# c in eight rows, turned and spread on chip, and 480 of 1920 low columns on GpSimd, in the first pass of a two-layer decoder

## Chip, core and metric

One core of a Trainium2 chip. The metric is the device time of one execution in microseconds; the kernel before takes 760.21 us (median of 3 runs, 759.72 to 760.39). The engines of the core run side by side and wait for each other through semaphores: TensorE (PE in the profile; PEld are its weight loads), VectorE (DVE), ScalarE (ACT), GpSimd (POOL) and SyncE (SP), which here issues most DMAs.

## What is computed

A decoder of two layers on one sequence of 256 tokens and width 1024, in float32. Each layer has a token mixer (layer 0: a mixture of three dilated attentions with 16 heads; layer 1: gated linear attention) and a gated convolutional FFN. Before each of them the input is normalised and modulated by shift and scale worked out from a conditioning vector `c`:

```python
mod = jax.nn.silu(c) @ w_ada[i] + b_ada[i]
sh1, sc1, g1, sh2, sc2, g2 = [m[:, None, :] for m in jnp.split(mod, 6, axis=-1)]
h = rmsnorm(x, norm_mix[i]) * (1.0 + sc1) + sh1
...
qkv = (h @ w_in).reshape(B, S, A_GROUPS, 3, A_HEADS, A_HEAD_DIM)
```

The change touches only the beginning: `silu(c)`, the norm of `x`, the first shift and scale, and the first part of `h @ w_in`.

## The kernel before

Everything is kept turned: channels on the 128 partitions, the 256 tokens along the free dimension, so `x` is eight tiles of 128 x 256 (`x_all`, `KT` = 8). A product of two float32 matrices is made from split operands: `hi` is the value rounded to a shorter format (`fp32r`), `lo` = value - `hi`, and three products hi·hi, lo·hi, hi·lo are summed (`mm3`, L200). For each weight tile ScalarE writes `hi` (a cast, `split`, L176) and VectorE writes `lo` (a subtraction of two SBUF operands, L182, or `low_part`, L188).

*Start (L85-126, L386-412).* `c` arrives as one row of 1024 numbers on one partition; two products with a row of ones (L125) spread it over all partitions, and ScalarE applies Silu from PSUM into `c_bc`, 128 x 1024, with the same numbers on every partition. Meanwhile `x` arrives in two halves, VectorE and ScalarE square it, VectorE adds the eight squares to two, TensorE sums over the channels, and ScalarE makes `rstd` from it through Ln and Exp (`rstd_of`, L212). Between these TensorE runs products that nobody reads (`keep_warm`, L297) and the six small products of the position bias (`rows`, L409).

*First pass (L415-440 and L673-685).* For each of the eight channel tiles `kt`:
- `ada_load` loads 128 x 2048 of `w_ada`, and two `ada_dot` (L138) on VectorE multiply one half each by `c_bc` and sum along the row; ScalarE turns each result into a shift or scale (`mod`, L150 or L152).
- `normed` (L282): VectorE writes `xr` = x · scale · rstd (L287), ScalarE `hhi` = round(xr + shift) (L289), VectorE `hlo` (L291).
- `split(..., lows=False)` (L165) loads 128 x 1920 of `w0`, and ScalarE casts two halves of 960; `low_part` (L185) is called once for each half on VectorE, the first behind `xr`, the second behind `hlo`.
- TensorE multiplies: 12 blocks of 128 columns for queries and keys (three products each, 256 columns) and a block of 384 for the values, for two halves of the tokens.

So VectorE's queue for one tile is: dot, dot, `xr`, low half, `hlo`, low half. Tiles 0 to 7 follow each other in it; `last` carries the order from tile to tile. The copies of `rows` from PSUM to SBUF (L437) stand on ScalarE behind the last cast of tile 0 (`copied[0]`).

*Order.* A scheduler places the instructions of each engine; `behind(i)` (L275) makes an instruction stand behind `i` in the queue of the same engine, and nothing between engines: real waits come from data and from buffers. A buffer of a pool is given out again once everything that uses it is done. PSUM has eight banks under three tags: 2 of `p`, 3 of `s`, 3 of `t`. `bank` (L74) takes the tag it is told, or the next from the cycle `p s t p s t s t`. Weight tiles have four raw buffers and three each for `hi` and `lo`.

Of the kernel before, what the change touches and what calls it, by code (L numbers as in the profile page):

```python
# [59 lines left out]
def trunk(ctx: ExitStack, tc: tile.TileContext, I, out):  # L60
# [16 lines left out]

    mm = nc.tensor.matmul

    def exp_ln_after(last):  # L80
        with tc.issue_after(last.ins):
            nc.scalar.preload_act_table_set(EXP_LN)


    c_row = wspl.tile([P, 2048], F32, tag="whi", name="c_row")  # L85
    nc.scalar.dma_start(c_row[:1, :D], I["c"])

    x_all = state.tile([P, KT, T], F32, name="x_all")
    x = [x_all[:, kt, :] for kt in range(KT)]

# [10 lines left out]
    def col(at):  # L101
        return small[:, at : at + 1]

    ones_d = const.tile([P, P], F32, name="ones_d")
    nc.vector.memset(ones_d, 1.0 / D)
    eps = const.tile([P, 1], F32, name="eps")
    nc.vector.memset(eps, EPS)
    ident = const.tile([P, P], F32, name="ident")
# [10 lines left out]
                                              op0=ALU.add, op1=ALU.mult)  # L119


    c_bc = const.tile([P, D], F32, name="c_bc")
    for n in range(2):
        ps = bank("cb", "t")
        last_c = mm(ps, ones_d[:1, :], c_row[:1, 512 * n : 512 * n + 512], start=True, stop=True)  # L125
        silu = nc.scalar.activation(c_bc[:, 512 * n : 512 * n + 512], ps, AF.Silu, scale=float(D))


    mod = {}
# [5 lines left out]
            nc.sync.dma_start(raw[:, c], I["w_ada"][l, n][:, c])  # L135
        return raw

    def ada_dot(l, n, s, raw):  # L138
# [3 lines left out]
        i = nc.vector.tensor_tensor_reduce(  # L142
            w, w, c_bc, op0=ALU.mult, op1=ALU.add, scale=1.0, scalar=0.0, accum_out=dot,
        )
        m = state.tile([P, 1], F32, tag=f"mod{l}{piece}{kt}", name="mod")
        b = col(C_BADA + 48 * l + 8 * piece + kt)
        if piece in (1, 4):
            g = col((C_NMIX if piece == 1 else C_NFFN) + 8 * l + kt)
            b1 = (16 if piece == 4 else 0) + 8 * l + kt
            j = nc.scalar.activation(m, dot, AF.Identity, scale=g, bias=one_b[:, b1 : b1 + 1])  # L150
# [120 lines left out]
    chain = {}  # L271
    squared = [None, None]

    @contextmanager
    def behind(*those):  # L275

        with ExitStack() as st:
            for i in those:
                st.enter_context(tc.issue_after(i.ins))
            yield  # L280

    def normed(l, sub, r, kt, first=(), between=None):  # L282

        xr = tmp.tile([P, T], F32, tag="xr", name="xr")
# [8 lines left out]
            )  # L293
        chain[kt] = chain[7] = i, j
        return h_hi[kt], h_lo[kt]

    def keep_warm(n):  # L297

        ps = bank("warm")
        for i in range(n):  # L300
            mm(ps[:, :P], ones_d, ones_d, start=True, stop=True)
# [82 lines left out]


    sq = wspl.tile([P, 2048], F32, tag="wlo", name="sq").rearrange("p (k t) -> p k t", k=KT)  # L386
    with behind(last_c):
        keep_warm(4)
    nc.vector.tensor_tensor(sq[:, 0:4, :], x_all[:, 0:4, :], x_all[:, 0:4, :], op=ALU.mult)
    with behind(silu):  # L390
        for i in (4, 6):
            last_sq = nc.scalar.activation(sq[:, i : i + 2, :], x_all[:, i : i + 2, :], AF.Square)
    for n in (0, 4):
        for m in (2, 1):
            last_add = nc.vector.tensor_tensor(sq[:, n : n + m, :], sq[:, n : n + m, :], sq[:, n + m : n + 2 * m, :], op=ALU.add)
        if n == 0:
            with behind(last_add):
                last_add = scale_terms(0)
    exp_ln_after(last_sq)
    r = rstd_of([sq[:, 0, :], sq[:, 4, :]])  # L400

    rows_ps, at = [], 0
    with behind(norm_ops[0]):
        keep_warm(3)
        for i, (g, n) in enumerate(ROWS):
            c = slice(at, at + n)
            ps = bank("rows", "t")[:16, 0:n]
            rows_ps.append((ps, c))
            last_row = mm(ps, tab[:, 16 * g : 16 * g + 16], oh[:33, c], start=True, stop=True)  # L409
            at += n  # L410
    with behind(last_row):
        keep_warm(6)


    w0, h = [], []  # L415
    last = last_add
    for kt in range(KT):
        ada = ada_load(0, kt, 1 if kt else 2)
        with behind(*((last,) if kt else (norm_ops[1], last))):
            dots = [ada_dot(0, kt, 0, ada)]  # L420
        with behind(dots[0][0]):
            dots.append(ada_dot(0, kt, 1, ada))

        def between(scaled, high):

            ahead, term = (dots[1][1], dots[1][1]) if kt == 0 else (dots[0][1], dots[1][1])
            w0.append(split(I["w0"][kt], 15 * P, 1 if kt else 2, after=((ahead,), (high,)), lows=False))
# [4 lines left out]
        with behind(chain[kt][1]):  # L432
            last = low_part(w0[kt], 1)
        if kt == 0:
            with behind(copied[0]):
                for ps, c in rows_ps:
                    nc.scalar.copy(rows[:, c], ps)  # L437
        if kt == 1:
            with behind(last):
                last = scale_terms(1)  # L440
# [35 lines left out]


    last_t, last_po, evacuated = [None], [None], []
    exps, norms, turned = [], [], []

    last_pv, last_s, last_cast = [], [None], [None]
    OLEVEL = (4, 5)
# [1 line left out]
    def scores(u, q, k, v, bias):  # L484
# [31 lines left out]
        for tiles in ((0, 1, 2), (3,)) if u == 0 else (range(4),):  # L516
            s = {i: bank("s", "t" if i == 3 and u else "s") for i in tiles}
            for i in tiles:
                with behind(*(last_pv if i or u > 1 else [])):
                    last = shared(s[i], i)  # L520
            for i in tiles:
                with behind(last):
                    ends = rest_of(s[i], i)
            last = ends
            with behind(last):
                last_s[0] = dilated(s, tiles)
            for i in tiles:
# [3 lines left out]
                nc.vector.tensor_tensor_reduce(  # L531
                    prob[i][:, 0:n], s[i][:, 0:n], back,
                    op0=ALU.add, op1=ALU.max, scale=1.0, scalar=-3e38, accum_out=m[:, i : i + 1],
                )
        pn = []

        def normalised():
# [6 lines left out]

        for hh in range(2):
            rs = slice(2 * hh, 2 * hh + 2)
            nc.vector.tensor_scalar(m[:, 4:8][:, rs], m[:, 0:4][:, rs], -1.0, None, op0=ALU.mult)
# [105 lines left out]
    for u in range(NPAIR):  # L653
# [13 lines left out]
        if u == 0:  # L667
            b0 = [bank("pqk", tg) for tg in "ssspp"]
            pqk = [b[:, T * i : T * i + T] for b in b0[:3] for i in range(2)]
            pv = b0[3:]  # L670
            b1 = [bank("pqk", "t") for _ in range(3)]
            pqk1 = [b[:, T * i : T * i + T] for b in b1 for i in range(2)]
            for kt in range(KT):  # L673
                s, e = kt == 0, kt == KT - 1

                for a, b in ((0, 0), (1, 0), (0, 1)):
                    for i in range(2 * NG):
                        w = parts(w0[kt], P * i)
                        mm(pqk[i], w[a], h[kt][b], start=s and i % 2 == 0 and (a, b) == (0, 0), stop=e and i % 2 == 1 and b == 1)
                wv = parts(w0[kt], 6 * P, NG * P)  # L680
                for a, b in ((0, 0), (1, 0), (0, 1)):
                    for t in range(2):
                        mm(pv[t][:, : NG * P], h[kt][a][:, P * t : P * t + P], wv[b], start=s and (a, b) == (0, 0), stop=e and b == 1)
                for i in range(2 * NG):
                    mm3(pqk1[i], parts(w0[kt], 9 * P + P * i), h[kt], s and i % 2 == 0, e and i % 2 == 1)
        if u < 2:
# [763 lines left out]
```

## Time and profile before

| | |
|---|---|
| median of 3 runs | 760.21 us (759.72 to 760.39) |
| profiled execution | 760.93 us, of which the span of the trace is 759.1 us |
| instructions | 16082 |
| first pass on TensorE | from 14.53 to 57.12 us of the span |
| VectorE in the first pass, mean of seven rounds | 5.33 us busy a round |
| GpSimd in the first 55 us | only memsets and the mask for `ident`, all before 1.5 us |

A row of the timeline has start, duration (both us), engine, line, operation, output <- inputs, shapes and how many instructions are merged; "[0.18 <-ACT hhi L289]" means that the engine sat idle for 0.18 us until ScalarE's write of `hhi` released it. VectorE's durations overlap a little with the next instruction's, so the pace is read from start to start. A row of the waits has who waited for whom, the total, how often, and the longest. A row of the DMA view has what is loaded, how many issues, KB each, and the time from issue to landing.

### The profile page before, as it was taken

Reading aid. Unit: us, or ns where it says so; the run is one execution under the profiler, and the core shown is the slowest. Engines: PE = TensorE matmul, PEld = TensorE weight load, DVE = VectorE, ACT = ScalarE, POOL = GpSimd, SP = SyncE. Lnnn points to the kernel's source line nnn. Section 1 sums busy time; section 2 is a strip of 40 time slices with the busy share of each in tenths; the row PEclk is TensorE's granted clock in tenths of the full one; section 3 lists DMA queues with packets and bytes.
Section 4 is the critical chain, followed back from the end, with each engine's and each line's share of the span. In section 5 each row is a group of like instructions: output and inputs, shape, how many; then the busy total and the mean of one; then the engine's idle time right before and its main releaser. Section 6 shows DMA issues by size and latency. Waiting matters only on the chain.

```text
span 759.1 us, 16082 instructions
## 1 busy us (share of the span) xinstructions
PE 750.4 (99%) x6416; PEld 732.7 (97%) x6416; DVE 650.8 (86%) x1195; ACT 485.7 (64%) x955; POOL 32.6 (4%) x57
## 2 busy tenths in 40 slices
PE   8999999999999999999999999999999999999997
PEld 6999999999999999999999999999999999999996
DVE  6998999899989778999999778887968999998592
ACT  5566676565556478676767556835967866676551
POOL 0001101101101010000000000000010000000100
PEclk9999999999999999999999999999999999999999
DMA  8988988878887357877746986864646777874621
GB/s 348 392 304 315 329 285 311 306 247 310 272 287 259 112 178 259 332 250 257 245 142 235 347 296 219 328 237 171 218 168 229 243 263 272 204 170 162 203 103 56
DMA packets 39481, 187.20 MB, mean 247 GB/s; under 512 B 9020, under 2 KB 11708, under 8 KB 25838
## 3 DMA queue, kind: packets, MB, share of 16 engines
q1 hardware_dynamic: 39024, 185.73, 70.4%
q8 instruction: 50, 0.82, 0.4%
q10 hardware_dynamic: 382, 0.45, 0.2%
q14 instruction: 25, 0.20, 0.1%
HBM read 185.06 MB, written 1.10 MB: 245 GB/s over the span
## 4 chain that ended last, share of the span: by engine, by line
PE 92%; DVE 4%; ACT 2%; issue 1%; DMA 0%; DVEq 0%; ACTq 0%
PE pab L203 10%; PE pab L204 10%; PE pab L205 10%; PE pqk L203 5%; PE pqk L205 5%; PE pd L203 5%; PE pd L204 5%; PE pd L205 5%; PE pqk L204 5%; PE pv L203 4%; PE pv L205 4%; PE pv L204 4%; PE py L203 2%; PE py L205 2%; PE py L204 2%; DVE ada_raw L142 2%
## 5 line engine op out<-in xcount | busy, mean ns | idle before, releaser
L176 ACT CAST whi<-raw 128x1024 fp32r<-128x1024 f32 (+4 forms) x264 | 237.9, 944 | 85.0 <-PE pab L204 34.2
L182 DVE TENSOR_TENSOR wlo<-raw,whi 128x1024 fp32r<-128x1024 f32 (+5 forms) x248 | 263.8, 1090 | 31.0 <-ACT whi L176 30.2
L204 PE MATMUL pab<-hlo,whi 128*128 128x256 f32 x672 | 184.8, 277 | 0.0
L205 PE MATMUL pab<-hhi,wlo 128*128 128x256 f32 x672 | 184.8, 276 | 0.0
L203 PE MATMUL pab<-hhi,whi 128*128 128x256 f32 x672 | 183.4, 277 | 0.0
L204 PEld LDWEIGHTS pab<-hlo,whi 128*128 128x128 f32 x672 | 126.1, 188 | 0.2
L205 PEld LDWEIGHTS pab<-hhi,wlo 128*128 128x128 f32 x672 | 126.1, 188 | 0.0
L203 PEld LDWEIGHTS pab<-hhi,whi 128*128 128x128 f32 x672 | 125.2, 188 | 0.1
L142 DVE CUSTOM_DVE_ANT_0 ada_raw<-ada_raw,c_bc 128x1024 f32<-128x1024 f32 x96 | 114.1, 1230 | 6.5 <-DMA ada_raw<-in_w_ada 6.3
L203 PE MATMUL pqk<-hhi,whi 128*128 128x256 f32 x356 | 97.9, 280 | 0.0
L204 PE MATMUL pqk<-hlo,whi 128*128 128x256 f32 x356 | 97.2, 278 | 0.0
L205 PE MATMUL pqk<-hhi,wlo 128*128 128x256 f32 x356 | 96.7, 279 | 0.0
L205 PE MATMUL pd<-ghi,wlo 128*128 128x256 f32 x308 | 84.8, 276 | 0.0
L204 PE MATMUL pd<-glo,whi 128*128 128x256 f32 x308 | 84.8, 276 | 0.0
L203 PE MATMUL pd<-ghi,whi 128*128 128x256 f32 x308 | 84.7, 276 | 0.0
L204 PEld LDWEIGHTS pqk<-hlo,whi 128*128 128x128 f32 x356 | 66.6, 188 | 0.1
L203 PEld LDWEIGHTS pqk<-hhi,whi 128*128 128x128 f32 x356 | 66.5, 188 | 0.1
L205 PEld LDWEIGHTS pqk<-hhi,wlo 128*128 128x128 f32 x356 | 65.9, 188 | 0.8 <-issue 0.7
L204 PEld LDWEIGHTS pd<-glo,whi 128*128 128x128 f32 x308 | 57.7, 188 | 0.0
L205 PEld LDWEIGHTS pd<-ghi,wlo 128*128 128x128 f32 x308 | 57.7, 188 | 0.0
L203 PEld LDWEIGHTS pd<-ghi,whi 128*128 128x128 f32 x308 | 57.7, 188 | 0.0
L203 PE MATMUL pv<-whi,hhi 128*128 128x384 f32 (+2 forms) x160 | 53.2, 338 | 0.3 <-ACT v L628 0.3
(271 smaller groups left out, 1498.5 us busy)
## 6 DMA issues: line engine op xcount, KB each, us to landing
raw<-in_w_up SPq DMA_DIRECT2D x42, 1024.0 KB, 5.0
ada_raw<-in_w_ada SPq DMA_DIRECT2D x29, 1024.0 KB, 5.8
raw<-in_w_down SPq DMA_DIRECT2D x28, 704.0 KB, 4.5
ada_raw<-in_w_ada SPq DMA_DIRECT2D x38, 512.0 KB, 6.7
raw<-in_wqk SPq DMA_DIRECT2D x18, 1024.0 KB, 6.4
raw<-in_wv SPq DMA_DIRECT2D x14, 768.0 KB, 6.2
raw<-in_w SPq DMA_DIRECT2D x7, 960.0 KB, 6.1
raw<-in_w_v_b SPq DMA_DIRECT2D x6, 768.0 KB, 5.7
```

The costliest lines, as they stand in the source:

```text
L142: i = nc.vector.tensor_tensor_reduce(w, w, c_bc, op0=ALU.mult, op1=ALU.add, scale=1.0, scalar=0.0, accum_out=dot,)
L176: copied[0] = nc.scalar.copy(part(hi[:, c]), part(raw[:, c]))
L182: last_lo[0] = nc.vector.tensor_tensor(part(lo[:, c]), part(raw[:, c]), part(hi[:, c].bitcast(F32)), op=ALU.subtract)
L203: mm(ps, a[0], b[0], start=start, stop=False)
L204: mm(ps, a[0], b[1], start=False, stop=False)
L205: return mm(ps, a[1], b[0], start=False, stop=stop)
```

## The change

1. `c` is loaded as eight rows of 128 on eight partitions. TensorE transposes it to 128 x 8, ScalarE applies Silu to that (`column`). VectorE multiplies the identity by each column (`spread`, two instructions of 512 columns), and two products with a matrix of 1/D spread it over the partitions; ScalarE copies them, times D, into `c_bc` (`keep_c`). The fill products are placed anew: 3, 2 and 1 around these steps and 5 behind `rows`, in place of 4, 3 and 6; all products of tile 0 for `pqk` and `pv` stand behind the last of them (`filled`). One tag of the cycle is skipped.
2. The squares: ScalarE takes two tiles of `x` in place of four, VectorE six, and four partial sums go to TensorE in place of two.
3. Tiles 0 and 1 cast their weights in three pieces (512, 448, 960 columns) in place of two halves, and VectorE makes the low part of the first two pieces one by one; for tile 0 VectorE works out the scale itself.
4. For every tile, the last 480 of 1920 columns of the low part are GpSimd's; VectorE keeps 960 to 1440.
5. At `u = 2`, the low parts of the first `wqk` tile stand behind two steps of the scores of `u = 0`.

```diff
-    c_row = wspl.tile([P, 2048], F32, tag="whi", name="c_row")
-    nc.scalar.dma_start(c_row[:1, :D], I["c"])
+    c_row = const.tile([KT, P], F32, name="c_row")
+    nc.scalar.dma_start(c_row, I["c"].rearrange("o (a b) -> (o a) b", a=KT))
...
+    def keep_warm(n, tag=None):
+        ps = bank("warm", tag)
+        for i in range(n):
+            last = mm(ps[:, :P], ones_d, ones_d, start=True, stop=True)
+        return last
+    last_c = keep_warm(3)
+    column = const.tile([P, KT], F32, name="column")
+    ps = bank("turned", "t")
+    with behind(last_c):
+        last_c = nc.tensor.transpose(ps[:, 0:KT], c_row, ident[0:KT, 0:KT])
+    silu = nc.scalar.activation(column, ps[:, 0:KT], AF.Silu)
+    exp_ln_after(silu)
+    with behind(last_c):
+        last_c = keep_warm(2)
+    spread = wspl.tile([P, 2048], F32, tag="whi", name="spread")[:, 0:D].rearrange("p (k c) -> p k c", k=KT)
     c_bc = const.tile([P, D], F32, name="c_bc")
-    for n in range(2):
-        ps = bank("cb", "t")
-        last_c = mm(ps, ones_d[:1, :], c_row[:1, 512 * n : 512 * n + 512], start=True, stop=True)
-        silu = nc.scalar.activation(c_bc[:, 512 * n : 512 * n + 512], ps, AF.Silu, scale=float(D))
+    c_ps = [bank("cb", "t") for _ in range(2)]
+    for i in range(2):
+        k = slice(4 * i, 4 * i + 4)
+        last = nc.vector.tensor_tensor(spread[:, k, :], ident.rearrange("p (o c) -> p o c", o=1).to_broadcast([P, 4, P]),
+                                       column[:, k].rearrange("p (k o) -> p k o", o=1).to_broadcast([P, 4, P]), op=ALU.mult)
+        with behind(last_c):
+            last_c = mm(c_ps[i], ones_d, spread[:, k, :].rearrange("p k c -> p (k c)"), start=True, stop=True)
+    with behind(last_c):
+        last_c = keep_warm(1)
+    def keep_c(n):
+        return nc.scalar.mul(c_bc[:, 512 * n : 512 * n + 512], c_ps[n], float(D))
...
+    with behind(last):
+        last = nc.vector.tensor_tensor(sq[:, 0:4, :], x_all[:, 0:4, :], x_all[:, 0:4, :], op=ALU.mult)
+    with behind(keep_c(0)):
+        last_sq = nc.scalar.activation(sq[:, 4:6, :], x_all[:, 4:6, :], AF.Square)
+    with behind(last):
+        last = add(0)
+    with behind(last_sq):
+        keep_c(1)
+    with behind(last):
+        last = square(6)
+    with behind(last):
+        last = add(4)
+    with behind(last):
+        last = scale_terms(0)
     with behind(last_c):
+        r = rstd_of([sq[:, i, :] for i in (0, 1, 4, 5)])
+    first_ada = ada_load(0, 0, 2)
+    next(cycle)
...
     with behind(last_row):
-        keep_warm(6)
+        filled = keep_warm(5)
...
+    CUTS, SHARED = (0, 512, 960, 1920), 1440
+    def second_low(w, *after):
+        hi, lo, raw, n = w
+        last_lo[0] = nc.gpsimd.tensor_tensor(lo[:, SHARED:1920], raw[:, SHARED:1920], hi[:, SHARED:1920].bitcast(F32), op=ALU.subtract)
+        with behind(*after):
+            return nc.vector.tensor_tensor(lo[:, n:SHARED], raw[:, n:SHARED], hi[:, n:SHARED].bitcast(F32), op=ALU.subtract)
...
+    def first_tiles(kt, last):
+        ada = ada_load(0, kt) if kt else first_ada
+        with behind(last):
+            dots = [ada_dot(0, kt, 0, ada, on_vector=kt == 0)]
...
+        with behind(dots[0][1] if kt else norm_ops[1]):
+            cast = piece(w, 0, 0)
+        with behind(dots[0][kt == 0], cast):
+            dots.append(ada_dot(0, kt, 1, ada))
+        def between(scaled, high):
+            with behind(scaled):
+                j = piece(w, 0, 1)
+            with behind(high):
+                i = piece(w, 1, 0)
+            with behind(i):
+                copied[0] = piece(w, 2, 0)
+            return [j]
+        with behind(dots[1][1]):
+            h.append(normed(0, 0, r, kt, (dots[1][0],), between))
+        last = chain[kt][1]
+        with behind(last):
+            last = piece(w, 1, 1)
+        return second_low(w, last)
+    for kt in range(2):
+        last = first_tiles(kt, last)
         if kt == 0:
             with behind(copied[0]):
                 for ps, c in rows_ps:
                     nc.scalar.copy(rows[:, c], ps)
...
+    for kt in range(2, KT):
...
+        h.append(normed(0, 0, r, kt, (dots[1][0],), between))
+        last = second_low(w0[kt], chain[kt][1])
...
-                w = split(I["wqk"][u - 2, g], 2048)
+                low, late = {(2, 0): (reduced[3:4], minus[1:2])}.get((u, g), ((), ()))
+                w = split(I["wqk"][u - 2, g], 2048, low=low, late=late)
...
-                        mm(pqk[i], w[a], h[kt][b], start=s and i % 2 == 0 and (a, b) == (0, 0), stop=e and i % 2 == 1 and b == 1)
+                        with behind(*([filled] if kt == 0 else [])):
+                            mm(pqk[i], w[a], h[kt][b], start=s and i % 2 == 0 and (a, b) == (0, 0), stop=e and i % 2 == 1 and b == 1)
```

`piece(w, i, op)` is ScalarE's cast (`op` 0) or VectorE's low part (`op` 1) of the columns `CUTS[i]` to `CUTS[i + 1]`. The last line of the diff stands in the same form for the products of `pv`.

More of the change, by code (lines that the diff above doesn't have):

```diff
@@ L78, in trunk, with behind @@
     mm = nc.tensor.matmul
+    @contextmanager
+    def behind(*those):
+        with ExitStack() as st:
+            for i in those:
+                st.enter_context(tc.issue_after(i.ins))
+            yield
     def exp_ln_after(last):
@@ L82, in exp_ln_after @@
             nc.scalar.preload_act_table_set(EXP_LN)
-    c_row = wspl.tile([P, 2048], F32, tag="whi", name="c_row")
-    nc.scalar.dma_start(c_row[:1, :D], I["c"])
+    c_row = const.tile([KT, P], F32, name="c_row")
+    nc.scalar.dma_start(c_row, I["c"].rearrange("o (a b) -> (o a) b", a=KT))
+    ones_d = const.tile([P, P], F32, name="ones_d")
+    nc.vector.memset(ones_d, 1.0 / D)
     x_all = state.tile([P, KT, T], F32, name="x_all")
@@ L102, in col @@
         return small[:, at : at + 1]
-    ones_d = const.tile([P, P], F32, name="ones_d")
-    nc.vector.memset(ones_d, 1.0 / D)
     eps = const.tile([P, 1], F32, name="eps")
@@ L136, in ada_load, with ada_dot @@
         return raw
-    def ada_dot(l, n, s, raw):
+    def ada_dot(l, n, s, raw, on_vector=False):
         piece, kt = ADA_ORDER[2 * n + s]
@@ L149, in ada_dot @@
             b1 = (16 if piece == 4 else 0) + 8 * l + kt
-            j = nc.scalar.activation(m, dot, AF.Identity, scale=g, bias=one_b[:, b1 : b1 + 1])
+            if on_vector:
+                j = nc.vector.tensor_scalar(m, dot, g, one_b[:, b1 : b1 + 1], op0=ALU.mult, op1=ALU.add)
+            else:
+                j = nc.scalar.activation(m, dot, AF.Identity, scale=g, bias=one_b[:, b1 : b1 + 1])
         else:
@@ L272, in trunk @@
     squared = [None, None]
[L274 to L280, printed above, removed]
     def normed(l, sub, r, kt, first=(), between=None):
@@ L295, in normed @@
         return h_hi[kt], h_lo[kt]
[L297 to L301, printed above, removed]
     early_x = [state.tile([P, T + 16], F32, tag=f"ex{k}", name="early_x") for k in range(KT)]
@@ L386, in trunk, with two, square, add @@
     sq = wspl.tile([P, 2048], F32, tag="wlo", name="sq").rearrange("p (k t) -> p k t", k=KT)
-    with behind(last_c):
[L388 to L400, printed above, removed]
+    def two(k):
+        return slice(k, k + 2)
+    def square(k):
+        return nc.vector.tensor_tensor(sq[:, two(k), :], x_all[:, two(k), :], x_all[:, two(k), :], op=ALU.mult)
+    def add(k):
+        return nc.vector.tensor_tensor(sq[:, two(k), :], sq[:, two(k), :], sq[:, two(k + 2), :], op=ALU.add)
+    with behind(last):
[12 more added lines that the diff above has]
+        last = scale_terms(0)
+    with behind(last_c):
+        r = rstd_of([sq[:, i, :] for i in (0, 1, 4, 5)])
+    first_ada = ada_load(0, 0, 2)
+    next(cycle)
     rows_ps, at = [], 0
     with behind(norm_ops[0]):
-        keep_warm(3)
         for i, (g, n) in enumerate(ROWS):
@@ L411, in trunk @@
     with behind(last_row):
-        keep_warm(6)
+        filled = keep_warm(5)
     w0, h = [], []
[L416 to L419, printed above, removed]
+    CUTS, SHARED = (0, 512, 960, 1920), 1440
[4 more added lines that the diff above has]
+            return nc.vector.tensor_tensor(lo[:, n:SHARED], raw[:, n:SHARED], hi[:, n:SHARED].bitcast(F32), op=ALU.subtract)
@@ new lines, in piece @@
+    def piece(w, i, op):
+        c = slice(CUTS[i], CUTS[i + 1])
+        hi, lo, raw, _ = w
+        if op:
+            return nc.vector.tensor_tensor(lo[:, c], raw[:, c], hi[:, c].bitcast(F32), op=ALU.subtract)
+        return nc.scalar.copy(hi[:, c], raw[:, c])
+    def first_tiles(kt, last):
+        ada = ada_load(0, kt) if kt else first_ada
+        with behind(last):
+            dots = [ada_dot(0, kt, 0, ada, on_vector=kt == 0)]
+        raw = wraw.tile([P, 2048], F32, tag="raw", name="raw")
+        for a, b in ((0, 1920),) if kt else ((0, 960), (960, 1920)):
+            last_load[0] = nc.sync.dma_start(raw[:, a:b], I["w0"][kt][:, a:b])
+        hi = wspl.tile([P, 2048], F32R, tag="whi", name="whi")
+        lo = wspl.tile([P, 2048], F32R, tag="wlo", name="wlo")
+        w = hi, lo, raw, 960
+        w0.append(w)
+        with behind(dots[0][1] if kt else norm_ops[1]):
[16 more added lines that the diff above has]
+        return second_low(w, last)
@@ L420, in trunk @@
+    for kt in range(2):
+        last = first_tiles(kt, last)
+        if kt == 0:
+            with behind(copied[0]):
+                for ps, c in rows_ps:
+                    nc.scalar.copy(rows[:, c], ps)
+    with behind(last):
+        last = scale_terms(1)
+    for kt in range(2, KT):
+        ada = ada_load(0, kt)
+        with behind(last):
             dots = [ada_dot(0, kt, 0, ada)]
@@ L424, in between @@
         def between(scaled, high):
-            ahead, term = (dots[1][1], dots[1][1]) if kt == 0 else (dots[0][1], dots[1][1])
-            w0.append(split(I["w0"][kt], 15 * P, 1 if kt else 2, after=((ahead,), (high,)), lows=False))
+            w0.append(split(I["w0"][kt], 15 * P, after=((dots[0][1],), (high,)), lows=False))
             with behind(scaled):
@@ L431, in trunk @@
         h.append(normed(0, 0, r, kt, (dots[1][0],), between))
[L432 to L440, printed above, removed]
+        last = second_low(w0[kt], chain[kt][1])
     with tc.issue_after(last_load[0].ins):
@@ L478, in trunk @@
     last_t, last_po, evacuated = [None], [None], []
-    exps, norms, turned = [], [], []
+    exps, norms, turned, reduced, minus = [], [], [], [], []
     last_pv, last_s, last_cast = [], [None], [None]
@@ L530, in scores @@
                 back = bass.AP(b.tensor, b.offset + n - 1, [b.ap[0], [-1, n]])
-                nc.vector.tensor_tensor_reduce(
+                reduced.append(nc.vector.tensor_tensor_reduce(
                     prob[i][:, 0:n], s[i][:, 0:n], back,
                     op0=ALU.add, op1=ALU.max, scale=1.0, scalar=-3e38, accum_out=m[:, i : i + 1],
-                )
+                ))
         pn = []
@@ L546, in scores @@
             rs = slice(2 * hh, 2 * hh + 2)
-            nc.vector.tensor_scalar(m[:, 4:8][:, rs], m[:, 0:4][:, rs], -1.0, None, op0=ALU.mult)
+            minus.append(nc.vector.tensor_scalar(m[:, 4:8][:, rs], m[:, 0:4][:, rs], -1.0, None, op0=ALU.mult))
             for r in (2 * hh, 2 * hh + 1):
@@ L682, in trunk @@
                     for t in range(2):
-                        mm(pv[t][:, : NG * P], h[kt][a][:, P * t : P * t + P], wv[b], start=s and (a, b) == (0, 0), stop=e and b == 1)
+                        with behind(*([filled] if kt == 0 else [])):
+                            mm(pv[t][:, : NG * P], h[kt][a][:, P * t : P * t + P], wv[b], start=s and (a, b) == (0, 0), stop=e and b == 1)
                 for i in range(2 * NG):
```

## The prediction

> **What bounds the kernel now.** I read the page first, then the first 60 us as waits of TensorE, as a timeline of its weight loads and of VectorE, and as windows of one VectorE round. The change lies in the first 58 us, all before or inside the pass over the tiles `w0` (L617-685).
>
> ```profile
> PE 750.4 (99%) x6416; PEld 732.7 (97%) x6416; DVE 650.8 (86%) x1195; ACT 485.7 (64%) x955; POOL 32.6 (4%) x57
> ```
>
> TensorE (PE) is busy 99% of the span, so a change counts only by where it moves TensorE's start of the pass or opens holes in it. These are the only two waits of its weight loads between 14 and 58 us:
>
> ```profile
> PEld pv L203 <- ACT v L628: 0.5, 1, 0.5
> PEld pqk L679 <- ACT hhi L289: 0.2, 1, 0.2
> ```
>
> And this is how it goes through the eight tiles (weight loads; the last row is the first product behind the pass):
>
> ```profile
> 14.53 0.78 PEld L679 LDWEIGHTS pqk<-hhi,whi 128*128 128x128 f32 x6
> ...
> 19.82 0.78 PEld L679 LDWEIGHTS pqk<-hhi,whi 128*128 128x128 f32 x6
> ...
> 25.11 0.78 PEld L679 LDWEIGHTS pqk<-hhi,whi 128*128 128x128 f32 x6
> ...
> 46.52 0.19 PEld L679 LDWEIGHTS pqk<-hhi,whi 128*128 128x128 f32 x1 [0.18 <-ACT hhi L289]
> ...
> 51.90 0.77 PEld L679 LDWEIGHTS pqk<-hhi,whi 128*128 128x128 f32 x6
> ...
> 57.12 0.19 PEld L496 LDWEIGHTS s<-q 128*128 128x128 f32 x1
> ```
>
> A tile costs TensorE 5.29 us (19.82 to 25.11). From 14.53 to 57.12 are 42.6 us, eight times 5.29 are 42.3: TensorE hardly waits. But VectorE is almost level with it. One round of VectorE, from the first dot product of a tile to that of the next:
>
> ```profile
> 21.29 1.22 DVE L142 CUSTOM_DVE_ANT_0 ada_raw<-ada_raw,c_bc 128x1024 f32<-128x1024 f32 x1
> ...
> 22.43 1.22 DVE L142 CUSTOM_DVE_ANT_0 ada_raw<-ada_raw,c_bc 128x1024 f32<-128x1024 f32 x1
> ...
> 23.58 0.48 DVE L287 SCALAR_TENSOR_TENSOR xr<-x_all,mod,rstd 128x256 f32<-128x256 f32 x1
> 23.98 1.15 DVE L188 TENSOR_TENSOR wlo<-raw,whi 128x960 fp32r<-128x960 f32 x1
> 25.05 0.48 DVE L291 SCALAR_TENSOR_TENSOR hlo<-xr,mod,hhi 128x256 fp32r<-128x256 f32 x1
> 25.58 1.16 DVE L188 TENSOR_TENSOR wlo<-raw,whi 128x960 fp32r<-128x960 f32 x1
> 26.65 1.22 DVE L142 CUSTOM_DVE_ANT_0 ada_raw<-ada_raw,c_bc 128x1024 f32<-128x1024 f32 x1
> ```
>
> Start to start these are 1.14 + 1.15 + 0.40 + 1.07 + 0.53 + 1.07 = 5.36 us, without a hole. Every one of them reads two full operands from SBUF. So VectorE's round is 0.07 us longer than TensorE's tile; at tiles 6 and 7 TensorE has caught up (46.52 waits for `hhi`). Whatever lengthens VectorE's round further is paid in full, tile for tile, and whatever shortens it gains next to nothing.
>
> **The change part by part: GpSimd beside VectorE.** For each tile 480 columns of the second low part go to GpSimd (POOL). What that does to VectorE is told by the few places where the two meet:
>
> ```profile
> 416.43 0.88 DVE L182 TENSOR_TENSOR wlo<-raw,whi 128x704 fp32r<-128x704 f32 x1
> ```
> ```profile
> 417.10 0.80 POOL L230 TENSOR_TENSOR sqacc<-sq 128x256 f32<-128x256 f32 x1 [143.26 <-ACT sq L227]
> ```
> ```profile
> 417.23 1.43 DVE L182 TENSOR_TENSOR wlo<-raw,whi 128x704 fp32r<-128x704 f32 x1
> ```
> ```profile
> 418.66 0.89 DVE L182 TENSOR_TENSOR wlo<-raw,whi 128x704 fp32r<-128x704 f32 x1
> ```
> ```profile
> 273.10 0.74 POOL L230 TENSOR_TENSOR sqacc<-sqacc,sq 128x256 f32<-128x256 f32 x1
> ```
>
> Three equal low parts of 704 columns: the first goes over to the second after 0.80 us, the second to the third after 1.43. In between GpSimd added two 256-column tensors (0.74 us where nothing disturbs it), and VectorE stood for 0.63 us. The same with the dot product, and with GpSimd as the one that waits first:
>
> ```profile
> 115.49 1.50 POOL L616 CAST q<-k 64x256 fp32r<-64x256 f32 x1
> ```
> ```profile
> 115.51 1.22 DVE L142 CUSTOM_DVE_ANT_0 ada_raw<-ada_raw,c_bc 128x1024 f32<-128x1024 f32 x1
> ...
> 116.65 1.41 DVE L142 CUSTOM_DVE_ANT_0 ada_raw<-ada_raw,c_bc 128x1024 f32<-128x1024 f32 x1
> ...
> 118.00 1.21 DVE L142 CUSTOM_DVE_ANT_0 ada_raw<-ada_raw,c_bc 128x1024 f32<-128x1024 f32 x1
> ```
>
> The cast stretches to 1.50 us because the dot holds it off until 116.65; then it gets in between two dots that follow without a gap, and the second takes 1.35 us to its successor instead of 1.14. So the two engines take turns, and GpSimd's turn is not skipped.
>
> *Saved on VectorE:* 704 columns take 0.80 us and 960 take 1.07, 1.05 ns a column; 480 take 0.56, which saves 1.07 - 0.56 = 0.51 us a tile. *Given back:* GpSimd's turn for 480 columns. No row shows that size. Below: 0.63 us, what 256 columns held. Above: the whole 0.74 scaled by 480/256, 1.39. Scaling the 0.63 gives 1.18; a small part of it will not grow with the columns, so I take **1.10**, near that. The round becomes 5.36 - 0.51 + 1.10 = **5.95 us** (bounds 5.48 and 6.24), 0.59 longer than before and 0.66 longer than TensorE's tile: the pass goes over to VectorE's pace.
>
> [...]
>
> **The start.** Rows used:
>
> ```profile
> 2.74 1.28 ACT L126 ACT_TABLE_LOAD   x1 [2.74 <-issue]
> ```
> ```profile
> 3.08 3.75 PE L125 MATMUL cb<-c_row,ones_d 1*128 1x512 f32 x4 [3.08 <-DMA c_row<-in_c]
> ```
> ```profile
> 9.60 1.22 DVE L142 CUSTOM_DVE_ANT_0 ada_raw<-ada_raw,c_bc 128x1024 f32<-128x1024 f32 x1
> ...
> 15.84 1.22 DVE L142 CUSTOM_DVE_ANT_0 ada_raw<-ada_raw,c_bc 128x1024 f32<-128x1024 f32 x1
> ```
> ```profile
> 6.87 0.60 ACT L126 ACTIVATE c_bc<-cb 128x512 f32<-128x512 f32 x1 [1.11 <-PE cb L125]
> ...
> 13.17 0.51 ACT L289 ACTIVATE hhi<-xr,mod 128x256 fp32r<-128x256 f32 x1
> 13.58 0.97 ACT L176 CAST whi<-raw 128x960 fp32r<-128x960 f32 x1
> 14.46 0.88 ACT L437 COPY rows<-rows 16x512 f32<-16x512 f32 x3
> ```
> ```profile
> 13.20 1.42 PEld L301 LDWEIGHTS warm<-ones_d 128*128 128x128 f32 x12 [0.21 <-issue]
> ```
> ```profile
> raw<-in_w SPq DMA_DIRECT2D x1, 480.0 KB, 7.3
> ```
> ```profile
> 4.96 0.33 SPq L169 DMA_DIRECT2D raw<-in_w  x1
> ```
> ```profile
> ada_raw<-in_w_ada SPq DMA_DIRECT2D x1, 1024.0 KB, 8.4
> ```
> ```profile
> 6.37 0.33 SPq L135 DMA_DIRECT2D ada_raw<-in_w_ada  x1
> ```
>
> c still lands near 3.08 (same 4 KB). The Silu of 128x8 must wait for the table (2.74 + 1.28 = 4.02), so `column` is there near 4.35 and the first `spread` (512 columns, 0.60) near 5.0. The two 512-column products ran at 0.85 us an instruction, 1.7 each; if still so they end near 8.45, and the last `keep_c` (0.60) near 9.25. The first dot moves from 9.60 to 9.25. Squares and `rstd` are no later (the four partial sums save two adds, the two `spread` cost as much). `hhi` no longer stands behind a 960-column cast on ScalarE but behind one of 512: another 0.5 us, so about 0.85 earlier, ready near 12.85 instead of 13.68. Two more casts follow (0.45 and 0.97; the second half of the tile has landed at 4.96 + 7.3 = 12.3): near 14.2 the second low part can begin, VectorE's 0.56 and GpSimd's 1.10 follow, and the dot of tile 1 starts near **15.85**, as before (15.84). It cannot start before its load lands, 6.37 + 8.4 = 14.8; later than 16.6 I see no reason for.
>
> *A new wait on TensorE.* Banks of tag `t` are three. The fifth `keep_warm` call asks for the sixth tag of the cycle, `t`, right behind three `rows` banks of that tag, and its bank comes free only when ScalarE has copied the first of them (L437), which stands behind the last cast of tile 0. That is 14.2 + 0.55 = 14.75. Then ten fill products (12 took 13.20 to 14.53, 0.111 each) 1.1 us: TensorE starts the pass near 15.9 instead of 14.53, with all of tile 0's products queued behind. At TensorE's own pace it would end at 15.9 + 42.3 = 58.2, 1.1 later than before.
>
> **The sum.** VectorE's path ends later than that, so it decides:
> - tile 0: 0 (-1.1 to +0.7).
> - tile 1, still in the form with three casts: 0.59, plus 0.33 waiting for the third cast (it ends 1.4 us behind `hhi` where the second ended 0.9 behind), plus 0.07 for one instruction more: +1.0.
> - tiles 2 to 6: 5 x 0.59 = +2.95 (5 x 0.12 to 5 x 0.88).
> - The start of tile 7 moves by 3.95, and with it `hhi` of tile 7, for which TensorE already waits now (51.90), and the end of the pass, 57.12 to 61.1.
> - Behind the pass, VectorE's low parts come 0.59 later against TensorE than now, and GpSimd's copies of k behind them; `s` and `pv` at 57.12 wait 0.47 us already. Half of it: +0.3 (0 to 0.6).
>
> Together +4.25 us (bounds +1.1, where TensorE's late start decides, and +7). All behind it is bound by TensorE and shifts. The rest costs nothing: the order of the low parts at `u = 2` lies under products of TensorE with no wait named, and the scale on VectorE for tile 0 is one column wide. The profiled execution took 760.93 us, 0.72 above the median: 765.2 profiled, **764.4** as a median.
>
> **Rivals.**
> - *No mutual exclusion that matters, late fill (A):* if GpSimd's turn holds VectorE under 0.44 us (4.85 + 0.44 = 5.29), TensorE's pace rules and only the bank counts: +1.1 - 0.2 for the two lost waits, **761.1**. For it: nothing; 0.63 was measured for half the columns.
> - *As meant (B), faster:* the same point, hold under 0.44 us, and a bank free for the fill. TensorE begins behind `hhi` at 12.85 and runs eight tiles unbroken to 55.2: -1.9, **758.3**. Against it: both rows above, and the bank count.
> - *Longer turn, slow TensorE (C):* 1.39 us a turn: 1.28 + 5 x 0.88 + 0.6, and the fill behind nearly 3 us of idle TensorE at twice the 0.111 us, as the products at 3.08 ran at half the later pace: +6.3, **766.5**. [...]
>
> **How the numbers follow.** Forecast 0.72, C 0.08, A 0.10, B 0.10. The forecast's own range is 762.6 to 766.0; down to A and up to C it is 761.0 to 766.8. What a measurement of this kernel can tell from no change is about 0.2%, 1.5 us: A lies within it, B is faster, the others slower: 0.10, 0.10, 0.80.
>
> **What would show it.** Right: low parts or dots of VectorE in the pass near 2.2 us instead of 1.2, once per tile; rounds near 5.95; from tile 3 or 4 on TensorE waiting 0.5 us or more for `hhi` per tile; `warm` loads behind the copy L437. Wrong: GpSimd's 480 columns beside unstretched VectorE rows; rounds under 5.3; the pass starting before 14.5; or holes behind 61 us, which would mean that the shift isn't all.

## The result, and the profile after

| | before | after |
|---|---|---|
| median | 760.3 us (759.72 to 761.2, 4 runs) | 765.92 us (765.46 to 766.83, 4 runs) |
| profiled execution, its span | 760.93, 759.1 us | 765.46, 763.7 us |
| ratio | 1 | 1.0065 (95%: 1.0038 to 1.0092) |

The change costs 4.5 us between the two profiled executions and 5.6 us between the medians (the quotient of these two medians, 1.0074, lies inside the interval of the ratio). It was forecast slower, at 764.4 us within 761.0 to 766.8.

VectorE's timeline after, one round in the pass (start, duration, engine, line, what):

```profile
33.62 2.24 DVE L174 CUSTOM_DVE_ANT_0 ada_raw<-ada_raw,c_bc 128x1024 f32<-128x1024 f32 x1
...
35.80 1.21 DVE L174 CUSTOM_DVE_ANT_0 ada_raw<-ada_raw,c_bc 128x1024 f32<-128x1024 f32 x1
...
36.95 0.47 DVE L314 SCALAR_TENSOR_TENSOR xr<-x_all,mod,rstd 128x256 f32<-128x256 f32 x1
37.34 1.15 DVE L223 TENSOR_TENSOR wlo<-raw,whi 128x960 fp32r<-128x960 f32 x1
38.41 0.47 DVE L318 SCALAR_TENSOR_TENSOR hlo<-xr,mod,hhi 128x256 fp32r<-128x256 f32 x1
38.95 0.66 DVE L454 TENSOR_TENSOR wlo<-raw,whi 128x480 fp32r<-128x480 f32 x1
39.53 2.25 DVE L174 CUSTOM_DVE_ANT_0 ada_raw<-ada_raw,c_bc 128x1024 f32<-128x1024 f32 x1
```

and GpSimd's row that belongs to its end:

```profile
39.05 1.64 POOL L452 TENSOR_TENSOR wlo<-raw,whi 128x480 fp32r<-128x480 f32 x1 [4.26 <-ACT whi L211]
```

The two halves of the low part are released together. VectorE takes the first turn (38.95). By the lengths of the rows, GpSimd waits behind it until about 39.6 and then works until 40.69 (39.05 + 1.64), and all that while the first dot of the next tile, started at 39.53, stands: 2.2 us instead of 1.2. Start to start it takes 2.18 us against 1.145 before: GpSimd's turn costs 1.03 us. The round is 39.53 - 33.62 = 5.91 us. The windows of VectorE by rounds (stretch, length, busy, granted clock, DMA share, GB/s) say the same for the others; the first holds two turns of GpSimd and the second none, since an instruction of 128x16 at 21.73, between the two, stood for the second turn (1.20 us; at 8.89 the same one takes 0.17):

```profile
15.38:22.85 7.47, 7.16 (x12) 0.77 1.01 402
22.85:27.71 4.86, 4.80 (x9) 1.00 0.93 323
27.71:33.62 5.91, 5.84 (x9) 1.00 0.91 342
...
45.43:51.32 5.89, 5.83 (x9) 1.00 0.92 343
```

TensorE after, its waits between 13 and 62.5 us (who waited for whom, total, times, longest) and its weight loads:

```profile
PEld warm L133 <- ACT rows L500: 3.0, 1, 3.0
PEld pqk L757 <- ACT hhi L316: 0.7, 2, 0.6
PEld s L573 <- POOL q L693: 0.4, 1, 0.4
```
```profile
12.02 0.31 PEld L441 LDWEIGHTS rows<-oh,tab 33*16 33x16 f32 x3 [0.34 <-issue]
15.30 1.19 PEld L133 LDWEIGHTS warm<-ones_d 128*128 128x128 f32 x10 [2.97 <-ACT rows L500]
16.41 1.35 PEld L757 LDWEIGHTS pqk<-hhi,whi 128*128 128x128 f32 x6
17.65 1.40 PEld L757 LDWEIGHTS pqk<-hhi,wlo 128*128 128x128 f32 x6
```
```profile
55.78 0.30 PEld L757 LDWEIGHTS pqk<-hhi,whi 128*128 128x128 f32 x2 [0.57 <-ACT hhi L316]
```
```profile
61.51 0.19 PEld L573 LDWEIGHTS s<-q 128*128 128x128 f32 x1 [0.44 <-POOL q L693]
```

The fill waits 2.97 us for the copy of `rows`, as the bank count said, and the pass starts at 16.41 instead of 14.53, although `hhi` of tile 0 is ready at 13.43. Six loads of tile 0 take 1.35 and 1.40 us where 0.78 was the rule. The windows of these stretches name the reason; behind the busy times of PE, PEld, DVE, ACT and POOL stands the granted clock:

```profile
12.60:15.30 2.70, 0.02 (x1) 0.00 (x0) 2.36 (x5) 2.67 (x7) 0.44 (x1) 1.00 1.01 419
15.30:16.41 1.11, 1.11 (x9) 1.11 (x10) 1.11 (x2) 0.26 (x2) 1.11 (x1) 1.00 1.02 420
16.41:19.80 3.39, 3.39 (x19) 3.39 (x18) 3.35 (x7) 1.73 (x5) 0.12 (x1) 0.51 1.00 407
```

The clock is granted in full for the fill and falls to half for the next 3.4 us, which costs TensorE 1.7 us. Every run comes with its mean granted clock: it is 0.994 to 0.997 in all four runs after, and never under 0.998 in the kernel before, so the fall is not one of the profiled execution alone. So there are two delays. By its own pace TensorE would end the pass at 16.41 + 42.3 + 1.7 = 60.4; VectorE, with `hhi` of tile 7 at 55.73 in place of 51.85, lets it end at 61.1. The experiments take the two apart.

That is not all. Behind the pass TensorE waits once more, for ScalarE's last copy of `v`, where the kernel before has no wait. The first weight load of `pv` behind the pass and the 97th, before and then after, with the wait that lies between them after:

```profile
57.78 0.19 PEld L203 LDWEIGHTS pv<-whi,hhi 128*128 128x128 f32 x1 [0.47 <-ACT v L628]
...
121.61 0.19 PEld L203 LDWEIGHTS pv<-whi,hhi 128*128 128x128 f32 x1
```
```profile
61.65 0.19 PEld L238 LDWEIGHTS pv<-whi,hhi 128*128 128x128 f32 x1
...
75.28 0.19 PEld L238 LDWEIGHTS pqk<-hhi,whi 128*128 128x128 f32 x1 [1.73 <-ACT v L705]
...
126.21 0.19 PEld L238 LDWEIGHTS pv<-whi,hhi 128*128 128x128 f32 x1
```

The shift is 3.87 us at the first of them and 4.60 at the second, and the span as a whole is 4.6 longer: the pass accounts for 3.9, and 0.7 are lost behind it. On ScalarE that last copy stands at 74.97, behind two exponentials (`prob`) and a copy of `pt`; in the kernel before it follows the other three copies directly (69.43). Why the scheduler placed it so was not looked into.

### The profile page after: what moved, and what is told of

The parts are those of the page before. It is cut to its first block, busy times and chain, and to the rows that moved or that the text cites. A ratio compares the mean times of both kernels' runs of the same rounds, so it can differ in the third digit from the quotient of the medians.

```text
span 763.7 us, 16113 instructions
## 1 busy us (share of the span) xinstructions
PE 751.5 (98%) x6417; PEld 734.4 (96%) x6417; DVE 656.9 (86%) x1199; ACT 485.4 (64%) x956; POOL 48.1 (6%) x65
## 4 chain that ended last, share of the span: by engine, by line
PE 92%; DVE 4%; ACT 2%; issue 1%; ACTq 0%; DVEq 0%
PE pab L239 10%; PE pab L240 10%; PE pab L238 10%; PE pqk L238 5%; PE pd L240 5%; PE pd L239 5%; PE pqk L240 5%; PE pd L238 5%; PE pqk L239 5%; PE pv L238 4%; PE pv L240 4%; PE pv L239 4%; DVE ada_raw L174 2%; PE py L238 2%; PE py L240 2%; PE py L239 2%
## 5 line engine op out<-in xcount | busy, mean ns | idle before, releaser
L211 ACT CAST whi<-raw 128x1024 fp32r<-128x1024 f32 (+5 forms) x260 | 234.1, 945 | 90.4 <-PE pab L239 37.5
L174 DVE CUSTOM_DVE_ANT_0 ada_raw<-ada_raw,c_bc 128x1024 f32<-128x1024 f32 x96 | 120.3, 1294 | 4.0 <-DMA ada_raw<-in_w_ada 3.6
L238 PE MATMUL pqk<-hhi,whi 128*128 128x256 f32 x356 | 99.8, 281 | 1.5 <-ACT v L705 1.5
L239 PE MATMUL pqk<-hlo,whi 128*128 128x256 f32 x356 | 98.9, 278 | 0.0
L240 PE MATMUL pqk<-hhi,wlo 128*128 128x256 f32 x356 | 98.5, 278 | 0.0
```

The source lines that it names most:

```text
L174: i = nc.vector.tensor_tensor_reduce(w, w, c_bc, op0=ALU.mult, op1=ALU.add, scale=1.0, scalar=0.0, accum_out=dot,)
L211: copied[0] = nc.scalar.copy(part(hi[:, c]), part(raw[:, c]))
L238: mm(ps, a[0], b[0], start=start, stop=False)
L239: mm(ps, a[0], b[1], start=False, stop=False)
L240: return mm(ps, a[1], b[0], start=False, stop=stop)
```

## The experiments

Nine kernels. The ratio is always to the kernel before, run beside each; it comes with its 95% interval.

| kernel | what | ratio | pass starts, ends on TensorE (us of the span) |
|---|---|---|---|
| before | | 1 | 14.53, 57.1 |
| after | | 1.0065 (1.0038 to 1.0092) | 16.41, 61.1 |
| a1 | after, low parts all on VectorE | 1.004 (1.0026 to 1.0055) | 16.30, 59.9 |
| a2 | after, fill in a free bank | 1.0071 (1.0053 to 1.0089) | 14.19, 61.7 |
| a3 | both of these | 1.0011 (0.9999 to 1.0022) | 12.98, 57.8 |
| a5 | a1, and products that bridge the gap | 1.0021 (1.001 to 1.0032) | 16.19, 58.5 |
| b1 | before, 480 columns on GpSimd | 1.0049 (1.0031 to 1.0067) | 14.38, 60.8 |
| b3 | before, 240 columns on GpSimd | 1.0036 (1.0024 to 1.0047) | 13.63, 58.5 |
| b2 | before, late fill | 1.0019 (1.0009 to 1.0029) | 17.40, 61.1 |
| c1 | a3, three casts in tile 0 only | 0.9998 (0.9988 to 1.0007) | 13.84, 57.1 |
| c2 | c1, order at u = 2 as before | 1.0007 (0.9998 to 1.0016) | 14.32, 57.6 |

**a1: GpSimd's share back on VectorE.**

```diff
-        last_lo[0] = nc.gpsimd.tensor_tensor(lo[:, SHARED:1920], raw[:, SHARED:1920], hi[:, SHARED:1920].bitcast(F32), op=ALU.subtract)
         with behind(*after):
-            return nc.vector.tensor_tensor(lo[:, n:SHARED], raw[:, n:SHARED], hi[:, n:SHARED].bitcast(F32), op=ALU.subtract)
+            last_lo[0] = nc.vector.tensor_tensor(lo[:, n:1920], raw[:, n:1920], hi[:, n:1920].bitcast(F32), op=ALU.subtract)
+        return last_lo[0]
```

> The changed kernel with GpSimd's 480 columns back on VectorE, all else kept (late fill too). Theory 'two delays, one behind the other': VectorE's round falls from 5.91 to about 5.4 us, so it no longer decides; but TensorE still starts tile 0 near 16.4 us of the span, runs it at half pace for some 3.4 us (1.65 us lost) and needs 8 x 5.29 = 42.3 for the pass: it ends near 60.4 instead of 61.0, so only 0.6 to 1.0 us come back: 3.4 to 4.0 us slower than before. Rival 'GpSimd alone': the whole loss comes back, within 0.5 us of before. Rival 'start alone': nothing comes back, 4.6 slower.

3.5 us between the medians (764.47 to 760.95). Its windows of all engines, one round, and TensorE's granted clock at the start of the pass, then its waits:

```profile
26.90:32.27 5.37, 5.37 (x46) 5.37 (x46) 5.31 (x10) 2.86 (x5) 0.00 (x0) 1.00 1.01 383
```
```profile
16.00:19.30 3.30, 3.30 (x18) 0.50 1.01 419
```
```profile
PEld warm L133 <- ACT rows L500: 3.0, 1, 3.0
PEld pv L238 <- ACT v L705: 0.9, 1, 0.9
```

VectorE is back at 5.37 us a round, TensorE does not wait for `hhi` once, and the pass still ends 2.8 us later than before: the late and slow start alone, which VectorE's delay had nearly covered. The nine executions have mean clocks of 0.993 to 0.998.

**a2: the fill in a free bank.** Tag `s`; the cycle is moved on by one, so that all later banks stay the same.

```diff
-        filled = keep_warm(5)
+        next(cycle)
+        filled = keep_warm(5, "s")
```

> The changed kernel with the fill products in a bank of tag s (free) instead of t, GpSimd's share kept. 'Two delays': TensorE starts the pass near 13.5 us at full pace instead of 16.4 at half pace, but then waits for hhi from tile 1 or 2 on, about 0.6 us a tile, and the pass ends where it ended, near 61.0: 4.3 to 4.7 us slower than before. 'Start alone': it would come out 3 us faster than the changed kernel, 1.5 slower than before. 'GpSimd alone': as 'two delays'.

Its waits of TensorE between 13 and 62.5 us:

```profile
PEld pqk L758 <- ACT hhi L316: 5.0, 7, 1.2
```

No gap, no slow products (mean clocks of 0.998 to 1.0 in its five executions), TensorE starts 2.2 us earlier than after, and waits it all away: for `hhi` at each of the seven further tiles, 0.5 to 1.2 us. The time stays that of the changed kernel: without the late fill, GpSimd's turns and the rest of the change are enough for the whole loss. But 6.0 us between the medians (766.93 to 760.95) are more than the 4.3 to 4.7 expected. The first load of `pv` is 4.4 us later than before, and with the same wait of 1.73 us behind the pass the profiled execution ends 6.0 later.

That loss behind the pass goes with GpSimd's share. From the first load of `pv` to the 97th the shift grows by 0.7 us in after, 1.6 in a2, 1.7 in b1 and 1.6 in b3, and by nothing in a1, a3 and a5 (c1, below, loses 0.5 by another wait). In a2 and b3 it is the same late copy of `v` as in after; b1 has other, shorter waits. No run moves that copy back, so what it costs by itself is not shown.

**a3: both undone.** The two edits together.

> Both undone: low parts on VectorE, fill in a free bank; the new path of c, the squares and the three casts of tiles 0 and 1 are kept. 'Two delays': VectorE's round is 5.37 again, the dot of tile 2 starts 0.4 us later than before (three casts in tile 1), the pass ends 0.0 to 0.6 us later than before: no change that can be told, -0.2 to +0.7 us. If the early start of TensorE were worth something by itself: 1.5 us or more faster than before.

About 1 us slower (761.98 to 760.95), more than the 0.7 expected at most; the interval just takes in no change. TensorE starts 1.5 us earlier than in the kernel before and has nothing of it:

```profile
PEld pqk L758 <- ACT hhi L316: 2.1, 3, 0.9
PEld pv L238 <- ACT v L706: 0.9, 1, 0.9
```

The longest of the three waits, 0.9 us for tile 6, lies behind a cast that waited 0.7 us for its load in the profiled execution; without it the pass would, by estimate, have ended near 57.1.

**b1: GpSimd's share in the kernel before.**

```diff
+    def second_low(w):
+        hi, lo, raw, n = w
+        last_lo[0] = nc.gpsimd.tensor_tensor(lo[:, 1440:1920], raw[:, 1440:1920], hi[:, 1440:1920].bitcast(F32), op=ALU.subtract)
+        return nc.vector.tensor_tensor(lo[:, n:1440], raw[:, n:1440], hi[:, n:1440].bitcast(F32), op=ALU.subtract)
...
-            last = low_part(w0[kt], 1)
+            last = second_low(w0[kt])
```

> The kernel before with only GpSimd's 480 columns added, start unchanged. VectorE stands 1.03 us a tile for 0.51 saved: rounds of 5.9 us; the start of tile 7 on VectorE moves by 7 x 0.53 = 3.7 us, less what TensorE's lead allows: 3.2 to 4.2 us slower than before. 'Start alone': no slower than before by more than 0.5.

A window of one round (PE, PEld, DVE, ACT, POOL busy) and the waits:

```profile
33.05:38.95 5.90, 5.50 (x44) 5.30 (x44) 5.84 (x10) 2.86 (x5) 1.65 (x2) 1.00 0.92 344
```
```profile
PEld pqk L684 <- ACT hhi L294: 4.0, 6, 0.9
```

The same 5.90 us rounds with the old start, and 4.2 us between the medians (765.17 to 760.95), the upper end of what was expected; the pass ends 3.7 us later than before. TensorE's loads fill 5.30 us of each round, the other 0.6 it waits.

**b3: half the columns.** As b1 with 1680 for 1440.

> The kernel before with 240 columns on GpSimd instead of 480. If VectorE stands as long as GpSimd works, by columns: 0.52 us a tile stood (half of 1.03) for 0.25 saved: rounds of 5.63 us, about 2 us slower than before. Rival 'a fixed price per GpSimd instruction': VectorE stands 0.9 us or more whatever the columns, rounds of 6.0 us or more, 4 us slower or more.

VectorE's timeline and GpSimd's, then the window of a round:

```profile
32.05 1.73 DVE L142 CUSTOM_DVE_ANT_0 ada_raw<-ada_raw,c_bc 128x1024 f32<-128x1024 f32 x1
...
33.71 1.22 DVE L142 CUSTOM_DVE_ANT_0 ada_raw<-ada_raw,c_bc 128x1024 f32<-128x1024 f32 x1
```
```profile
31.32 1.37 POOL L193 TENSOR_TENSOR wlo<-raw,whi 128x240 fp32r<-128x240 f32 x1 [4.25 <-ACT whi L176]
```
```profile
32.05:37.68 5.63, 5.50 (x44) 5.30 (x43) 5.58 (x10) 2.86 (x5) 1.38 (x2) 1.00 0.99 358
```

The dot stands 33.71 - 32.05 - 1.145 = 0.52 us, half of 1.03 for half the columns: VectorE pays 2.15 ns for each column that GpSimd takes and saves 1.05. If that holds between and below these two sizes, there is no share at which this gains; others were not run. The rounds are 5.63 us, as expected; the time (3.0 us between the medians) is 1 us above the expectation. In the profiled execution the shift is 1.3 us at the first load of `pv` and 2.9 behind the wait for the last copy of `v`, 1.73 us at 72.71.

**b2: the late fill in the kernel before.**

```diff
-        keep_warm(6)
+        next(cycle)
+        filled = keep_warm(6, "t")
...
+                        with behind(*([filled] if kt == 0 else [])):
+                            mm(pqk[i], w[a], h[kt][b], ...)
```

> The kernel before with its last fill products in a bank of tag t and tile 0's products queued behind them, nothing else. The fill waits for the copy of rows, about 15.1 us of the span. If the gap of TensorE (13.3 to 15.1, 1.8 us) leaves it at full pace, the pass starts at 16.4 and ends at 58.7: 1.6 us slower. If it falls to half pace as in the changed kernel: another 1.2 (fill) and 1.7 (pass), 3.5 to 4.5 slower. VectorE's rounds stay at 5.37.

```profile
PEld warm L301 <- ACT rows L439: 2.5, 1, 2.5
```

TensorE's windows (stretch, length, PE busy, granted clock, DMA share, GB/s):

```profile
12.60:14.90 2.30, 0.05 (x2) 0.71 0.99 409
...
15.05:20.18 5.13, 5.13 (x25) 0.50 1.01 420
```

Neither expectation fits both the profile and the time. The gap came out longer (2.5 us), and in the profiled execution the clock fell to half within it and stayed there for 5.1 us of work; the pass ends 3.9 us later than before, and that execution is the slowest of ten, 764.0 us. The median of the ten is 762.79, only 1.5 us above before (761.25). As far as the mean clock tells, executions without a fall are not the reason: it is 0.995 to 0.997 in seven of the ten and 0.999 in three, and these three (762.61, 763.36 and 763.81 us) are not faster than the seven (median 762.56). What half a clock costs this kernel in time stays open.

**a5: the gap bridged.** On a1, 13 calls more of the fill product in bank `s` between `rows` and the late fill.

```diff
+        last_row = keep_warm(13, "s")
+    with behind(last_row):
         filled = keep_warm(5)
```

> As a1 (low parts on VectorE, fill late), but 13 more products that nobody reads, in a free bank, stand between rows and the late fill, so that TensorE doesn't sit idle for 3 us. If the slow products of tile 0 come from that gap: the pass starts near 16.4 all the same, but at full pace, and ends 1.5 to 1.7 us earlier than in a1: 1.5 to 2.2 us slower than before. If the slow pace had another cause: as a1, 3.2 to 3.8 slower.

```profile
12.18 4.09 PEld L133 LDWEIGHTS warm<-ones_d 128*128 128x128 f32 x36 [0.21 <-issue]
16.19 0.77 PEld L759 LDWEIGHTS pqk<-hhi,whi 128*128 128x128 f32 x6
```
```profile
16.20:19.80 3.60, 3.60 (x31) 1.00 1.01 422
```

The pass starts as late as in a1, but the clock stays full, six loads take 0.77 us, and the pass ends 1.4 us earlier. The ratio falls from 1.004 to 1.0021, and none of the twelve executions has a mean clock under 0.998. The two intervals overlap a little; with the profiles beside them, about half of a1's loss is the clock and the rest the lateness itself.

**c1 and c2: what is left of a3.** c1 runs `first_tiles` for tile 0 alone (`range(1)`) and tile 1 in two halves; c2 also takes `low` and `late` at `u = 2` away.

> As a3 (low parts on VectorE, fill in a free bank), with the three casts only in tile 0 and tile 1 in two halves as before. Tile 1's round on VectorE falls from 5.92 to 5.45 us, tile 2 starts 0.4 us earlier than in the kernel before (in a3 it starts when it did there): -0.6 to +0.3 us against before, and 0.4 to 0.6 faster than a3. Rival: the three casts cost nothing in tile 1, no difference to a3.

> As c1, but the low parts of the first wqk tile stand as in the kernel before (part 5 of the change undone). The pass ends as in c1, within 0.5 us of before. If that order costs nothing, as the prediction took it: no difference to c1, -0.7 to +0.5 us against before. If the 0.5 to 0.9 us that c1 loses between 57 and 95 us of the span come from it: 0.5 to 0.9 us faster than c1 and before.

c1 is the kernel before in time, within 0.1%; its tile 7 has `hhi` at 51.75 us (before: 51.85). Each against the kernel before beside it, c1 is 1.0 us better than a3, though the two intervals overlap. Tile 1's round falls from 5.92 to 5.46 us, as expected, but tile 2 starts at 21.53, 0.2 us later than before and not 0.4 earlier, because the dot of tile 1 starts at 16.07 (15.40 in a3). c2 is not told from c1: the times show no gain from the old order at `u = 2`, though in the profiles c1 loses 0.5 us from the first load of `pv` to the 97th and c2 0.2. In both, TensorE waits longer for `v` there than in the kernel before (0.47); the rows are those of c1:

```profile
PEld pv L238 <- ACT v L707: 0.9, 1, 0.9
PEld pqk L759 <- ACT hhi L316: 0.3, 1, 0.3
```

No version here is faster than the kernel before.

## Why the prediction was right, and where its numbers were off

- **The turn-taking of VectorE and GpSimd, the step that decides: right.** Taken: 1.10 us a tile, a round of 5.95. Measured: 1.03 and 5.90 (b1). The fixed part that I kept in the scaled value was an estimate of mine, and 480 and 240 columns show none (1.03 and 0.52 us, b3). What put 1.10 too high is the row it was scaled from: 0.63 us for 256 columns are 2.46 ns a column, and it was 2.15.
- **Tile 0: mis-sized.** Taken as 0, with the dot of tile 1 at 15.85 behind GpSimd's turn. The second low part starts at 14.81 us instead of 14.2, and the dot of tile 1, started at 15.38, stands for 1.01 us, as if it had started at 16.39: +0.55 against 15.84. Of ScalarE's timeline after:

```profile
11.26 0.47 ACT L252 ACTIVATE ln<-ms,eps 128x256 f32<-128x256 f32 x1 [1.82 <-PE ms L250]
11.77 0.42 ACT L254 ACTIVATE rstd<-ln 128x256 f32<-128x256 f32 x1
...
12.92 0.51 ACT L316 ACTIVATE hhi<-xr,mod 128x256 fp32r<-128x256 f32 x1
```

  `rstd` comes 0.27 us later than before (11.50), not "no later": ScalarE waits for TensorE's sum over the squares, whose eight products (9.03 to 11.23) stand behind the second product of c and a fill. So `hhi` is ready at 13.43 and not at 12.85. The first dot, 9.47, was near its 9.25.
- **Tile 1: right.** +1.0 taken; the round without the turn of tile 0 is 22.85 - 16.39 = 6.46 against 5.45. a3 and c1 show the three casts' part: 5.92 against 5.46.
- **Tiles 2 to 6: too large.** +2.95 taken, +2.3 measured. The turn accounts for a part (5 x 0.54 = 2.7), and the rest is a hole that the kernel before has and after has not, in the sixth round of seven (5.70 against 5.37):

```profile
42.77:48.47 5.70, 5.70 (x47) 5.52 (x46) 5.31 (x9) 2.87 (x5) 0.00 (x0) 1.00 0.99 395
```

- **The sum.** `hhi` of tile 7 moved by 55.73 - 51.85 = 3.88 us; 3.95 was forecast. Two errors, +0.55 and -0.6, met in it: that the sum of the pass came out to 0.1 us is luck.
- **Behind the pass: mis-sized, and the forecast's own sign of it came.** +0.3 taken, for `s` and `pv`. The 0.44 us that `s` waits for GpSimd's copies of k only replace the 0.47 of `pv` before; what is lost is the hole of 1.73 us at 75.28, net 0.7. "All behind it is bound by TensorE and shifts" does not hold there, and "holes behind 61 us" was named as what would show that. The span is 4.6 us longer (4.25 forecast). The medians lie 1.1 us further apart than the profiled executions; 765.46 is the lowest of the four runs after. What the runs vary by was not settled; the highest, 766.83, has the lowest mean clock (0.994).
- **The bank: right, but I made too little of it.** The wait, its place and its cause were as forecast. The prediction had TensorE end at 58.2 by its own pace and kept the half clock for rival C, with the fill slow. The fill ran at full pace and tile 0 at half, so TensorE's own end was 60.4, and VectorE's came only 0.7 us after it. That is why a1 gives back so little, and why another sign failed: TensorE was to wait 0.5 us or more per tile from tile 3 or 4 on, and it waits twice, at tiles 6 and 7, for 0.7 us in all. Where it starts early (a2) it waits at every tile. The rows that C leaned on for a half clock, the slow products at 3.08, do not show one: the windows of the kernel before grant 1.00 from 2 to 6 us.
- **Rivals.** The measured 765.92 us lies nearer to C (766.5) than to the forecast (764.4), but C's turn of 1.39 us did not come, and the slow products came in tile 0 and not in the fill, without deciding the end of the pass. A and B needed a turn under 0.44 us; it was 1.03. B's other half, an early start of TensorE, was tried in a3 and c1: it gains nothing as long as VectorE's round is 5.37.

## What to carry to other kernels

In this kernel a subtraction moved from VectorE to GpSimd, both reading two operands from SBUF, is not off VectorE's path: price the stand of VectorE at what GpSimd's turn takes (here 2.15 ns a column against 1.05 saved), and move such work only where VectorE idles. Look for new waits behind the part that was changed, too: in the kernels with GpSimd's share they cost 0.7 to 1.7 us. Where two engines are within 0.1 us a round of each other, undo suspects one by one and together: a1 and a2 alone each leave most of the loss. Count buffers by tag also for fill products that nobody reads: this one held up the whole pass for a bank.

## What was not expected of the hardware

TensorE's clock fell after 2.97 us without a weight load (2.7 without a product), and not in the gap: the ten fill products ran at full pace (0.111 us each), and only then did 3.4 us at a granted clock of 0.51 follow. In b2 it fell within a gap of 2.5 us (0.71 granted on average from 12.60 to 14.90 us) and work ran at 0.50 for 5.1 us; as far as the mean clocks tell, it fell in seven of the ten executions (0.995 to 0.997) and not in the other three (0.999). So a gap of 2.5 us is not always safe in this kernel. What sets the moment of the fall was not shown, and how long a safe gap may be was not measured.

GpSimd also got its turn between VectorE instructions that follow without a hole, tile after tile: its rows last 1.64 to 1.70 us in after, 0.6 to 0.7 more than the turn of 1.03, which is the length of the low part (0.66) that VectorE had under way.
